# Weights of three projections shifted by 32 bytes in longer buffers, in a decoder layer on one core

## The chip, the cores and the metric

The kernel runs on one core of a Trainium2 chip. The metric is the device time of one execution in microseconds (us); lower is better. A profiled execution gives a trace of every instruction beside that time.

## The reference, cut to what matters

A decoder layer on x of 256 tokens by 1024 features, all in float32:

```
h = rmsnorm(x) ; proj = h @ w_in                       # 1024 -> 3*512 + 512 + 2*1024
q, k, v, u_pool, gate_logits = split(proj)
attn   = causal attention of 8 heads of 64 (one block of 256 tokens), q and k normed and rotated
pooled = causal trailing means of u_pool over 2, 4, 8, 16 tokens, minus the token, a linear map per group
x  = x + (sigmoid(gate_0) * (attn @ w_branch_attn) + sigmoid(gate_1) * (pooled @ w_branch_pool)) @ w_out
up = conv3(rmsnorm(x) @ w_up)                           # 1024 -> 2 * 2816, depthwise, causal
out = x + (silu(gate half of up) * value half of up) @ w_down
```

## The kernel before

Each float32 operand of a large matmul is split in two tiles of type float32r: `hi`, the value rounded (ScalarE, `high`, L80), and `lo`, the rest (VectorE, `low`, L84). A product is then three matmuls: hi by hi, hi by lo, lo by hi. That goes for the weights as well as for the activations.

Weights come in chunks of 128 partitions by 2048 columns (8 KB on each partition), in the order of the list `order` (L97 to L107): q, k, v, p, g, pool, bp, ba, o, up, dn. q's weights come together with x in the tile `xq`; the other chunks are loaded into `raw` buffers by SyncE's queue (`load`). `next_high` and `next_low` split a chunk by pieces, some pieces ahead of TensorE; `next_high` also takes the two tiles for a new chunk, `his[c]` and `los[c]`, from two pools of four buffers each, `whi` and `wlo` (L147 and L148). The sequence of instructions on every engine is the order in which the Python code issues them, and it is kept as written.

Two ways of multiplying matter here:

- `project` (L278) makes q, k and v, token by token: the activation tiles `xhi` and `xlo` are the stationary operand (128x128) and the weights are the moving operand, 512 columns at a time. For each of q, k and v there are 8 steps of k, 3 products and 2 halves of the tokens: 48 matmuls, 144 in all. They come first in the program.
- All other large matmuls (`mm3`, L92 to L94, and `down`, L635 to L637) have the weights as the stationary operand (128x128) and the activations as the moving operand, 256 columns at a time. They are 2460.

Where the tiles lie: each partition holds, one behind the other, the small constants, four `raw` buffers, four `whi`, four `wlo`, and then the activations, of which `xq` is the first. Constants, `raw`, `whi` and `wlo` buffers that matter here begin on a multiple of 64 bytes: `whi` at byte 56768, and each next buffer 8192 further. `xq` has eight columns of `norm_mix_g` (32 bytes) ahead of x and is 24608 bytes long, which is 32 bytes more than a multiple of 64; so x and every activation tile behind it (`xhi` at byte 146912, `xlo`, `qkT`, `vn`, the pooled and attention tiles, those of the FFN) begin 32 bytes behind a multiple of 64. In every float32r matmul of this kernel the two operands so have starts that differ by 32 bytes within 64: the weights at 0, the activations at 32.

Of the kernel before, what the change touches and what calls it, by code (L numbers as in the profile page):

```python
# [9 lines left out]
F32R = mybir.dt.float32r  # L10
# [4 lines left out]
P = 128  # L15
# [17 lines left out]
CH = 2048  # L33
# [19 lines left out]
FFN_AHEAD = 6  # L53
KREADY = 1
FIRST = 2
XCUTS = (1, 2, 4, 6, 8)


@with_exitstack
def hybrid_layer_kernel(ctx: ExitStack, tc: tile.TileContext, xq_d, par_d, wkv_d, wpg_d,  # L60
# [5 lines left out]
    whi_p = ctx.enter_context(tc.tile_pool(name="whi", bufs=WBUFS))  # L66
    wlo_p = ctx.enter_context(tc.tile_pool(name="wlo", bufs=WBUFS))
# [11 lines left out]
    def high(hi, src, scale=1.0):  # L79
        nc.scalar.activation(hi, src, AF.Copy, scale=scale)  # L80
# [16 lines left out]
    order = [("q", None)] * 2 + [("k", wkv_d[c]) for c in range(2)]  # L97
# [10 lines left out]
    raws, his, los = {}, {}, {}  # L108
# [14 lines left out]
    def raw(c, sl):  # L123

        return xq[:, 4 * c + sl.start // 512, S:] if order[c][0] == "q" else raws[c][:, sl]
# [10 lines left out]
    def oldest():  # L136

        return next((c for c in range(len(order)) if c not in spent), len(order))

    def next_high():  # L140
        if at[0] < len(pieces):
            c, sl, first, _ = pieces[at[0]]
            if c - oldest() >= WBUFS:
                return
            at[0] += 1
            if first:
                his[c] = whi_p.tile([P, CH], F32R, tag="whi", name=f"hi_{order[c][0]}{c}")  # L147
                los[c] = wlo_p.tile([P, CH], F32R, tag="wlo", name=f"lo_{order[c][0]}{c}")  # L148
            high(his[c][:, sl], raw(c, sl))

    def next_low(eager=False):
# [9 lines left out]
    def ahead(upto=0):  # L161

        next_high()
        next_low()
        if at[1] - sum(p[0] < used[0] for p in pieces) < upto:
            next_high()
            next_low()
# [23 lines left out]
    cut = 0  # L191
    for k in XCUTS:
        end = KD + k * (S + AW)
# [25 lines left out]
    for k in range(KD):  # L219
        if k == 0:  # L220
            nc.vector.tensor_scalar(xhi[:, k, :], xT[:, k, :], gmix[:, k:k + 1], None, op0=ALU.mult)
        else:
            high(xhi[:, k, :], xT[:, k, :], gmix[:, k:k + 1])
        low(xlo[:, k, :], xhi[:, k, :], xT[:, k, :], gmix[:, k:k + 1])
        next_high()
        next_low(eager=True)
# [83 lines left out]
    def to_heads(qg, t, dst, name):  # L310
        pq = bank(f"ps_t{name}{t}")
        flat = qg.rearrange("p h d -> p (h d)")
        for j in range(KA):
            nc.tensor.transpose(pq[:, j * P:(j + 1) * P], flat[:, j * P:(j + 1) * P], ident)
        nc.scalar.activation(dst[:, :, t * P:(t + 1) * P], pq.rearrange("p (j c) -> p j c", c=P), AF.Copy)
# [110 lines left out]
    def scores(hp):  # L426
        ps = ps2.tile([P, 2, 512], F32, tag="ps2", name=f"ps_s{hp}")
        for j in range(2):
            rows = slice(j * DH, (j + 1) * DH)
            nc.tensor.matmul(ps[:, j, P:3 * P], qT[rows, hp, P:S], kT[rows, hp, :], start=True, stop=True)  # L430
            nc.tensor.matmul(ps[:, j, 0:P], qT[rows, hp, 0:P], kT[rows, hp, 0:P], start=True, stop=True)
        sm = tmp.tile([P, 2, 3 * P], F32, tag="big", bufs=4, name=f"sm{hp}")
        nc.vector.tensor_tensor(sm, ps[:, :, 0:3 * P],
                                mask.rearrange("p a b -> p (a b)")[:, None, :].to_broadcast([P, 2, 3 * P]), ALU.add)
        mx = tmp.tile([P, 2, 2], F32, tag="mx", name=f"mx{hp}")
        for t in (1, 0):
            nc.vector.tensor_reduce(mx[:, t, :], sm[:, :, TOK[t]], axis=AX.X, op=ALU.max)
        nc.vector.tensor_scalar(mx, mx, -(DH ** -0.5), None, op0=ALU.mult)
        sums = tmp.tile([P, 2, 2], F32, tag="sums", name=f"sums{hp}")
        for j in range(2):  # L440
            for t in (1, 0):
                nc.scalar.activation(sm[:, j, TOK[t]], sm[:, j, TOK[t]], AF.Exp, bias=mx[:, t, j:j + 1],
                                     scale=DH ** -0.5, accum_out=sums[:, t, j:j + 1])
        rs = tmp.tile([P, 2, 2], F32, tag="rs", name=f"rs{hp}")
        nc.vector.reciprocal(rs, sums)
        for t in (1, 0):
            n = TOK[t].stop - TOK[t].start
            nc.gpsimd.tensor_tensor(sm[:, :, TOK[t]], sm[:, :, TOK[t]],
                                    rs[:, t, :, None].to_broadcast([P, 2, n]), ALU.mult)
        later(4, weigh, hp, sm)  # L450
# [46 lines left out]
    for n in range(2 * KD):  # L497
        if n == KREADY:
            for t in range(NT):
                to_heads(kg[t], t, kT, "k")  # L500
        if n >= FIRST and (n - FIRST) % 4 == 0:
            scores((n - FIRST) // 4)
        if n == 10:
            pool_maps()
            ahead()
        b, c = n // 2, n % 2
# [267 lines left out]
```

## Time and profile before

| | |
|---|---|
| median of 3 runs | 350.35 us (348.51 to 350.55) |
| profiled execution, its own time | 348.69 us |
| its span, first to last instruction | 346.9 us |
| outside the span | 1.8 us |
| mean granted TensorE clock | 1.000 |

The profile gives for each engine the time it was busy in the span (PE is TensorE's matmuls, PEld its weight loads, DVE VectorE, ACT ScalarE, POOL GpSimd), a strip of 40 slices, the chain of work that ended last, and groups of equal instructions. A matmul's own duration includes a latency that the next matmul overlaps: how fast TensorE gets on is read from the distance between the starts of two matmuls, not from the duration of one.

### The profile page before, as it was taken

To read this page: it belongs to the slowest core of one execution; us is meant where nothing else is said; L and a number is where in the kernel's file an instruction comes from. 1 tells how busy PE (TensorE), PEld (TensorE's weight loads), DVE (VectorE), ACT (ScalarE), POOL (GpSimd) and SP (SyncE) were. 2 spreads that over 40 slices of the span, in tenths; PEclk is the share of its full clock that TensorE was granted. 3 is DMA by queue.
4 is the path that set the end of the run, shared out by engine and by line. 5 is a ranking of instruction groups with operands and counts; after the bars stand their busy time and mean duration, and the time that the engine had idled before them with its cause. 6 is when DMAs were issued, how large, how long until landed. Compare 5 with 4: busy or idle time off the path is not lost.

```text
span 346.9 us, 6715 instructions
## 1 busy us (share of the span) xinstructions
PE 340.7 (98%) x2736; PEld 329.2 (95%) x2736; DVE 261.0 (75%) x411; ACT 195.7 (56%) x311; POOL 101.5 (29%) x111
## 2 busy tenths in 40 slices
PE   8999999999999999999999999999999999999996
PEld 6887899999899999999999999999999999999995
DVE  4969889787587585899699877776777777777643
ACT  4956534634748945665367655555555555646420
POOL 1007991112202034586232212121212121212230
PEclk9999999999999999999999999999999999999999
DMA  7985642465272651566257555464636363652003
GB/s 275 419 327 213 222 159 110 150 220 213 69 259 92 242 201 45 175 237 211 109 168 271 188 224 201 164 222 145 242 123 243 131 235 132 232 162 83 0 2 121
DMA packets 10254, 62.76 MB, mean 181 GB/s; under 512 B 1136, under 2 KB 2288, under 8 KB 3312
## 3 DMA queue, kind: packets, MB, share of 16 engines
q1 hardware_dynamic: 10224, 62.34, 49.5%
q8 instruction: 21, 0.34, 0.4%
q14 instruction: 9, 0.07, 0.1%
HBM read 61.29 MB, written 1.05 MB: 180 GB/s over the span
## 4 chain that ended last, share of the span: by engine, by line
PE 80%; DVE 10%; DMA 4%; ACT 2%; issue 2%; SPq 1%; POOL 0%; ACTq 0%
PE ps_up L93 11%; PE ps_up L94 11%; PE ps_up L92 11%; PE ps_d L636 6%; PE ps_d L637 6%; PE ps_d L635 6%; PE ps_g L92 4%; PE ps_g L94 4%; PE ps_g L93 4%; DMA raw_k<-in_wkv 4%; PE ps_v L278 3%; DVE lo_up L84 2%; DVE hlo L86 2%; PE ps_bp L92 1%; PE ps_ba L94 1%
## 5 line engine op out<-in xcount | busy, mean ns | idle before, releaser
L92 PE MATMUL ps_up<-hhi,hi_up 128*128 128x256 f32 x352 | 98.5, 280 | 0.0
L93 PE MATMUL ps_up<-hlo,hi_up 128*128 128x256 f32 x352 | 98.4, 279 | 0.1
L94 PE MATMUL ps_up<-hhi,lo_up 128*128 128x256 f32 x352 | 98.3, 279 | 0.0
L93 PEld LDWEIGHTS ps_up<-hlo,hi_up 128*128 128x128 f32 x352 | 66.2, 188 | 0.4 <-DVE hlo L86 0.4
L92 PEld LDWEIGHTS ps_up<-hhi,hi_up 128*128 128x128 f32 x352 | 66.2, 188 | 0.0
L94 PEld LDWEIGHTS ps_up<-hhi,lo_up 128*128 128x128 f32 x352 | 66.2, 188 | 0.0
L84 DVE TENSOR_TENSOR lo_up<-raw_up,hi_up 128x1024 fp32r<-128x1024 f32 x44 | 55.9, 1273 | 6.1 <-ACT hi_up L80 6.1
L618 POOL TENSOR_TENSOR c_v<-c_g,c_v 128x256 f32<-128x256 f32 x22 | 16.2, 738 | 120.8 <-DVE c_v L601 120.8
L636 PE MATMUL ps_d<-al,hi_dn 128*128 128x256 f32 x176 | 49.1, 279 | 0.0
L635 PE MATMUL ps_d<-ah,hi_dn 128*128 128x256 f32 x176 | 49.1, 279 | 0.0
L637 PE MATMUL ps_d<-ah,lo_dn 128*128 128x256 f32 x176 | 49.1, 279 | 0.0
L80 ACT ACTIVATE hi_up<-raw_up 128x1024 fp32r<-128x1024 f32 x44 | 44.9, 1045 | 0.0
L92 PE MATMUL ps_g<-xhi,hi_g 128*128 128x256 f32 x128 | 36.5, 285 | 0.0
L93 PE MATMUL ps_g<-xlo,hi_g 128*128 128x256 f32 x128 | 35.7, 279 | 0.0
L94 PE MATMUL ps_g<-xhi,lo_g 128*128 128x256 f32 x128 | 35.7, 279 | 0.0
L80 ACT ACTIVATE ah<-c_v 128x256 fp32r<-128x256 f32 x22 | 9.2, 418 | 45.8 <-POOL c_v L618 45.8
L637 PEld LDWEIGHTS ps_d<-ah,lo_dn 128*128 128x128 f32 x176 | 33.1, 188 | 0.0
L635 PEld LDWEIGHTS ps_d<-ah,hi_dn 128*128 128x128 f32 x176 | 33.1, 188 | 0.0
L636 PEld LDWEIGHTS ps_d<-al,hi_dn 128*128 128x128 f32 x176 | 33.1, 188 | 0.0
L606 DVE TENSOR_TENSOR u_v<-ps_up,R 128x256 f32<-128x256 f32 x22 | 9.3, 421 | 26.1 <-PE ps_up L94 26.1
L84 DVE TENSOR_TENSOR lo_dn<-raw_dn,hi_dn 128x1024 fp32r<-128x1024 f32 x22 | 27.8, 1264 | 0.4 <-ACT hi_dn L80 0.4
L642 POOL TENSOR_TENSOR al<-c_v,ah 128x256 fp32r<-128x256 f32 x22 | 23.0, 1045 | 11.6 <-ACT ah L80 11.6
(182 smaller groups left out, 815.8 us busy)
## 6 DMA issues: line engine op xcount, KB each, us to landing
raw_up<-in_wup SPq DMA_DIRECT2D x22, 1024.0 KB, 4.8
raw_dn<-in_wdn SPq DMA_DIRECT2D x11, 1024.0 KB, 4.8
raw_g<-in_wpg SPq DMA_DIRECT2D x8, 1024.0 KB, 4.8
raw_o<-in_wout SPq DMA_DIRECT2D x4, 1024.0 KB, 4.8
xq<-in_xq SPq DMA_DIRECT2D x3, 768.0 KB, 7.4
raw_v<-in_wkv SPq DMA_DIRECT2D x2, 1024.0 KB, 14.1
raw_p<-in_wpg SPq DMA_DIRECT2D x2, 1024.0 KB, 6.3
raw_bp<-in_wbp SPq DMA_DIRECT2D x2, 1024.0 KB, 4.8
```

Source lines behind the costliest of these rows:

```text
L80: nc.scalar.activation(hi, src, AF.Copy, scale=scale)
L84: nc.vector.tensor_tensor(lo, src, hi.bitcast(F32), ALU.subtract)
L92: nc.tensor.matmul(out, sh, mh, start=start, stop=False, **kw)
L93: nc.tensor.matmul(out, sh, ml, start=False, stop=False, **kw)
L94: nc.tensor.matmul(out, sl, mh, start=False, stop=stop, **kw)
L278: nc.tensor.matmul(pt[t], sx[:, k, t * P:(t + 1) * P], wx[:, sl], start=k == 0 and sx is xhi and wx is hi, stop=k == KD - 1 and wx is lo)
L606: nc.vector.tensor_tensor(u, ps[:, 0:S], R2, ALU.mult)
L618: nc.gpsimd.tensor_tensor(uc[1], g[1], uc[1], ALU.mult)
L635: nc.tensor.matmul(o, hi[:, sl], acch[i], start=first, stop=False, skip_group_check=True)
L636: nc.tensor.matmul(o, hi[:, sl], accl[i], start=False, stop=False, skip_group_check=True)
L637: nc.tensor.matmul(o, lo[:, sl], acch[i], start=False, stop=i == KF - 1, skip_group_check=True)
L642: nc.gpsimd.tensor_tensor(accl[i], act_i, acch[i].bitcast(F32), ALU.subtract)
```

## The change

`BEHIND` is a number of float32 columns. The tiles of all weights are made 16 columns (64 bytes) longer, and for chunks of q, k and v the part that is used begins 8 columns (32 bytes) behind the tile's start; all others use the tile from its start.

```
+BEHIND = 8
...
             if first:
-                his[c] = whi_p.tile([P, CH], F32R, tag="whi", name=f"hi_{order[c][0]}{c}")
-                los[c] = wlo_p.tile([P, CH], F32R, tag="wlo", name=f"lo_{order[c][0]}{c}")
+                name = order[c][0]
+                off = BEHIND if name in ("q", "k", "v") else 0
+                his[c] = whi_p.tile([P, CH + 2 * BEHIND], F32R, tag="whi", name=f"hi_{name}{c}")[:, off:off + CH]
+                los[c] = wlo_p.tile([P, CH + 2 * BEHIND], F32R, tag="wlo", name=f"lo_{name}{c}")[:, off:off + CH]
             high(his[c][:, sl], raw(c, sl))
```

No instruction is added, removed or moved on any engine, and no wait: row for row the two programs differ in nothing but their source lines, which are 1 higher after L56 and 3 more after L148 (L80 becomes L81, L278 becomes L282). Nor does a tile change its buffer. What changes is where they lie. The eight weight buffers follow each other by 8256 bytes in place of 8192, so that all still begin on a multiple of 64; `xq` and all tiles behind it move up by 512 bytes (`xhi` from 146912 to 147424) and still begin 32 bytes behind a multiple of 64. q's, k's and v's weights now begin at 32 too, as the stationary tiles `xhi` and `xlo` do that they are multiplied with. For the other 2460 matmuls the operands stay 32 bytes apart within 64, but their distance in whole steps of 64 bytes changes, by between 1 and 8 steps, by the buffer.

## Rows read from the trace of the kernel before

**Rows 1.** The page: busy time of each engine, and the granted clock by slices.
```profile
PE 340.7 (98%) x2736; PEld 329.2 (95%) x2736; DVE 261.0 (75%) x411; ACT 195.7 (56%) x311; POOL 101.5 (29%) x111
...
PEclk9999999999999999999999999999999999999999
```
**Rows 2.** The page: the chain that ended last, by engine.
```profile
PE 80%; DVE 10%; DMA 4%; ACT 2%; issue 2%; SPq 1%; POOL 0%; ACTq 0%
```
**Rows 3.** Waits of TensorE's matmuls: total us, times, longest.
```profile
PE ps_warm L204 <- DVE ones L178: 1.0, 1, 1.0
PE ps_s L430 <- ACT qkT L315: 0.5, 1, 0.5
PE ps_q L278 <- ACT hi_q L80: 0.4, 2, 0.3
PE ps_n L249 <- DVE diag L245: 0.4, 1, 0.4
PE ps_v L278 <- DVE qg_q L291: 0.3, 1, 0.3
```
**Rows 4.** Timeline of TensorE, q to p: start us, us, instruction, count.
```profile
9.77 0.63 PE L278 MATMUL ps_q<-lo_q,xhi 128*128 128x512 f32 x2
...
17.24 0.63 PE L278 MATMUL ps_k<-hi_k,xhi 128*128 128x512 f32 x2
...
28.84 0.63 PE L278 MATMUL ps_k<-lo_k,xhi 128*128 128x512 f32 x2
29.31 0.40 PE L278 MATMUL ps_v<-hi_v,xhi 128*128 128x512 f32 x1
30.02 0.47 PE L278 MATMUL ps_v<-hi_v,xhi 128*128 128x512 f32 x1 [0.31 <-DVE qg_q L291]
30.33 0.63 PE L278 MATMUL ps_v<-hi_v,xlo 128*128 128x512 f32 x2
...
40.59 0.63 PE L278 MATMUL ps_v<-lo_v,xhi 128*128 128x512 f32 x2
41.06 0.28 PE L92 MATMUL ps_u<-xhi,hi_p 128*128 128x256 f32 x1
```
**Rows 5.** Timeline of TensorE in the FFN's up projection, 15 steps of three.
```profile
200.66 0.28 PE L92 MATMUL ps_up<-hhi,hi_up 128*128 128x256 f32 x1
...
205.92 0.28 PE L92 MATMUL ps_up<-hhi,hi_up 128*128 128x256 f32 x1
```
**Rows 6.** Groups: matmuls and weight loads; the first number behind the bar is busy us, then mean ns.
```profile
L93 PE MATMUL ps_up<-hlo,hi_up 128*128 128x256 f32 x352 | 98.4, 279 | 0.1
...
L93 PEld LDWEIGHTS ps_up<-hlo,hi_up 128*128 128x128 f32 x352 | 66.2, 188 | 0.4 <-DVE hlo L86 0.4
...
L635 PE MATMUL ps_d<-ah,hi_dn 128*128 128x256 f32 x176 | 49.1, 279 | 0.0
...
L278 PE MATMUL ps_v<-lo_v,xhi 128*128 128x512 f32 x16 | 5.0, 396 | 0.0
...
L278 PEld LDWEIGHTS ps_v<-lo_v,xhi 128*128 128x128 f32 x16 | 3.0, 188 | 0.7
```
**Rows 7.** Writers of four weight tiles and two activation tiles: ns min/median/max, first and last start.
```profile
L84 DVE TENSOR_TENSOR lo_q<-xq,hi_q x8: 684/685/693, 5.2 to 13.7; 128x512 fp32r<-128x512 f32 x8
L84 DVE TENSOR_TENSOR lo_k<-raw_k,hi_k x4: 1216/1218/1225, 14.4 to 22.6; 128x1024 fp32r<-128x1024 f32 x4
L84 DVE TENSOR_TENSOR pooll<-pl,poolh x4: 393/418/421, 53.5 to 67.5; 128x256 fp32r<-128x256 f32 x4
L80 ACT ACTIVATE hi_q<-xq x8: 615/616/629, 4.4 to 12.8; 128x512 fp32r<-128x512 f32 x8
L80 ACT ACTIVATE hi_k<-raw_k x4: 1042/1044/1061, 13.3 to 19.0; 128x1024 fp32r<-128x1024 f32 x4
L80 ACT ACTIVATE ah<-c_v x22: 417/418/419, 170.9 to 335.6; 128x256 fp32r<-128x256 f32 x22
```

## The prediction

> **What bounds the kernel now.** I read the busy times first, then the chain that ended last, then TensorE's waits, and last the starts of single matmuls. TensorE's matmuls cover 340.7 of 346.9 us, at a granted clock that the strip shows as 9 tenths or more in every slice [rows 1], which is the level of 2.4 GHz; 80% of the chain is TensorE's [rows 2]. Its waits are few: five rows of 0.3 to 1.0 us, and only two of them, 0.4 us for q's first weights and 0.3 us at v's start, lie in the part where q, k and v are made [rows 3]. So the time is the number of matmuls times the distance between their starts, and a change of that distance is what could move it.
>
> That distance is read from starts. In q's last 32 matmuls it is (17.24 - 9.77) / 32 = 233.4 ns; in v's last 46 it is (41.06 - 30.33) / 46 = 233.3 ns [rows 4]. In the up projection it is (205.92 - 200.66) / 45 = 116.9 ns [rows 5]. The first kind moves 512 columns, the second 256, so both take 0.456 ns for a column. At the granted 2.4 GHz a column of one cycle would take 0.417 ns (512 of them 213.3 ns): each matmul carries 9% above that, 20 ns in 512 columns and 10 ns in 256.
>
> **The change, part by part.**
>
> *The start of the moving operand.* This is the part that could work on TensorE directly: 144 matmuls read their moving operand, the weights, from 32 bytes behind a multiple of 64 in place of 0. The kernel before has both cases side by side: weights that move in q, k and v start at 0 [rows 4], activations that move in the up projection start at 32 [rows 5], and a column takes the same 0.456 ns. The mean durations say the same by another way: 396 ns for 512 columns less 279 ns for 256 is 117 ns for 256 columns [rows 6]. The 9% grows with the columns and not with the matmuls, so it is not an extra line at the start that another offset would save or add. Term: 144 x 0 ns = 0.
>
> *The pair of starts.* What no row of before shows is a float32r matmul whose two operands start alike within 64 bytes; after the change q, k and v are such. Bounds from both sides: at best the 9% goes from all 144, 144 x 20 = 2.9 us; at worst each load of a stationary tile, now hidden under the matmul ahead of it, has to be waited for, 144 x 188 ns = 27 us [rows 6]. I take 0, the value nearest to the rows: a load takes 188 ns whether its tile starts at 0 (ps_up) or at 32 (ps_v), and if loads and moving reads disturbed each other, the excess would come once for each load; but a matmul of 512 columns has one load just as one of 256 has, and twice the excess.
>
> *The writers.* ScalarE and VectorE now write 16 pieces each of q, k and v at offset 32. VectorE takes 684 ns for 512 columns with a source at 32 and the rest at 0, and 1218 ns for 1024 with everything at 0: the difference, 534 ns, is that of 512 columns, so what is left for the start is 151 ns in both. With all three tiles at 32 the fastest of 256 columns is 393 ns and the median 418, again some 151 ns above half of 534 [rows 7]. ScalarE: 1044 less 616 ns is 428 ns for 512 columns and leaves 188 ns for the start; 256 columns from 32 to 32 took 418 ns, which leaves 204 [rows 7]. So at most 16 ns on 16 pieces, 0.26 us, on an engine that is busy 56% of the span [rows 1] and that delayed q's matmuls twice by 0.4 us together [rows 3]. Only the first pieces of q, with x just arriving, are uncovered. Term: 0 to 0.05 us.
>
> *The longer buffers.* The 2460 other matmuls keep their operands 32 bytes apart within 64, and only whole steps of 64 bytes between them change. They are most of the time, so a nanosecond on each would be 2.5 us. Bounds: the whole excess gone or doubled, 2460 x 10 = 24.6 us either way. I take 0: ps_up and ps_d read different activation tiles against all the weight buffers, and both have 279 ns [rows 6]. That is weak, since by the addresses all these distances are whole kilobytes and 32 bytes; what speaks more for 0 is again that the excess follows the columns and not the loads.
>
> No instruction, queue or wait moves, so nothing is late in another place. Sum against the profiled execution: 348.69 + 0 (0 to 0.05). That execution lies 1.7 us under the median of the runs, inside their spread of 348.51 to 350.55; I forecast the median, unchanged: **350.3 us**, its own range 348.4 to 351.0.
>
> **The rivals.**
>
> *A: operands that start alike lose the excess.* The 144 matmuls then come every 213 ns. For it: 20 ns on each are unexplained by the columns at the granted clock, and every pair that shows them starts 32 bytes apart. Against it: two opposite arrangements, 0 against 32 and 32 against 0, give one and the same 0.456 ns. The gain would mostly be lost again: in q and k together it is at most 96 x 20 = 1.9 us, but v's second matmul starts at 30.02 when VectorE has cleared the bank of q's second half [rows 4, 3], and VectorE's sequence does not get earlier. What is sure is v's part, 46 x 20 = 0.9 us: 350.35 - 0.9 = 349.4, and 347.4 if the wait fell too.
>
> The Trainium skill states for it, in "TensorE: Matmul & The Clock Gate", section "Wait — 56ns, not 53.3ns?", that warm matmuls start N / 2.4 + 2.5 ns apart, 215.8 ns at 512 columns, which the page measured with another type. The trace disagrees, with 233.3 ns. If the page's distance came back with the new start, the gain would be 17.5 ns on each, 0.8 us for v's 46.
>
> *B: operands that start alike get into each other's way.* The load for the next matmul runs while this one moves its columns; with the same phase both could ask for the same part of the memory in the same cycle. Place: the 144 matmuls of q, k and v. Price: if the load's 128 columns each cost the moving side one column's time, 128 x 0.417 = 53 ns, 144 x 53 = 7.7 us, so 358.0. It decides from 24 ns a matmul (3.5 us). For it: the pair is new in this kernel. Against it: the excess does not come once per load, as told.
>
> The Trainium skill speaks against it too: "SBUF — State Buffer", section "Who interferes with whom", gives TensorE two read ports, one for the moving operand and one for weight loads, independent of each other. By that the price is 0. That loads of 188 ns at 116.9 ns between matmuls cost no more per column than at 233.3 agrees; a pair in phase is shown by no run here.
>
> *C: whole steps of 64 bytes count.* Then the longer buffers change the 2460 others, and the sign is open: 1 ns on each is 2.5 us, 352.8 or 347.9; it decides from 1.4 ns. For it: their number. Against it: the equal rows of ps_up and ps_d, as far as they go, and that the excess does not follow the loads.
>
> **How the numbers follow.** No change 0.74; A 0.10; B 0.07; C 0.09. One per cent, about what a measurement of this kernel can tell from no change, is 3.5 us. A stays below it by its own arithmetic, but for 0.02 together with a low draw of the runs; C gives 0.04 to each side; of B 0.06 is above the bound. Faster by over 1%: 0.02 + 0.04 = 0.06. Slower: 0.06 + 0.04 = 0.10. Within 1%: 0.84. The range reaches down to A's better end and, for a weak B or C, up to 353: 347.5 to 353.0. It leaves out most of B and of C, some 0.14.
>
> **What would show it.** Right: matmuls of q, k and v still 233 ns apart, those of the up projection 117, loads at 188, and v's start at about 30 us with its wait on VectorE. A would show as 213 to 216 ns in q, k and v, with a longer wait at v's start; B as 250 ns or more there, with p starting later than 41 us; C as a distance other than 117 ns in the FFN, perhaps in one buffer of four. The forecast is wrong if any of these distances moved by more than 2%.

## The result, and the profile after

| | before | after |
|---|---|---|
| median | 350.19 us (348.44 to 350.59, 8 runs) | 351.88 us (351.77 to 352.11, 8 runs) |
| ratio, 95% interval | | 1.0062 (1.0043 to 1.0081) |
| span of the profiled execution | 346.9 us | 350.2 us |

The change is slower by some 0.6%. That is less than the 1% that the prediction took for what a measurement can tell from no change, and yet it is clear of noise, since the interval does not hold 1. One thing is needed to read the sizes: the kernel before has two times, one near 348.7 and one near 350.3 us, and its median falls on one or the other by the set of runs; the changed kernel has one time. The profiled execution of before was one of the shorter (348.69 us), so that the two profiles differ by 3.3 us where these medians differ by 1.7. The ratios, here and below, weigh the runs of both times and so are not the quotients of the medians beside them. Where the two times come from is shown by the ninth experiment.

The page of the changed kernel, busy times and granted clock:

```profile
PE 344.0 (98%) x2736; PEld 332.6 (95%) x2736; DVE 261.1 (75%) x411; ACT 195.7 (56%) x311; POOL 102.1 (29%) x111
...
PEclk9999999999999999999999999999999999999999
```

Against [rows 1], TensorE is busy 3.3 us longer, which is the whole difference of the spans, and VectorE, ScalarE and GpSimd are busy as long as before, within 0.6 us. The clock is the same. So TensorE's own work became longer. Its waits in the changed kernel (us in total, times, longest) add up to 2.9 us where those of [rows 3] add up to 2.6. The difference lies at q's first weights, and it is made up again before p starts, as the timeline below shows:

```profile
PE ps_warm L207 <- DVE ones L181: 1.1, 1, 1.1
PE ps_q L281 <- ACT hi_q L81: 0.7, 2, 0.4
PE ps_s L433 <- ACT qkT L318: 0.4, 1, 0.4
PE ps_v L281 <- DVE qg_q L294: 0.4, 1, 0.4
PE ps_n L252 <- DVE diag L248: 0.3, 1, 0.3
```

The timeline of TensorE from q to p (start us, us, instruction, count), the part whose tiles were shifted. L281 is L278 of the kernel before: the lines behind L148 are 2 higher, not 3, than those ahead of it, and the section on the change is wrong there.

```profile
9.82 0.62 PE L281 MATMUL ps_q<-lo_q,xhi 128*128 128x512 f32 x2
...
17.26 0.62 PE L281 MATMUL ps_k<-hi_k,xhi 128*128 128x512 f32 x2
...
29.23 0.40 PE L281 MATMUL ps_v<-hi_v,xhi 128*128 128x512 f32 x1
30.01 0.47 PE L281 MATMUL ps_v<-hi_v,xhi 128*128 128x512 f32 x1 [0.39 <-DVE qg_q L294]
...
30.78 0.62 PE L281 MATMUL ps_v<-lo_v,xhi 128*128 128x512 f32 x2
...
34.86 0.62 PE L281 MATMUL ps_v<-lo_v,xhi 128*128 128x512 f32 x2
...
35.78 0.63 PE L281 MATMUL ps_v<-hi_v,xlo 128*128 128x512 f32 x2
...
40.91 0.28 PE L93 MATMUL ps_u<-xhi,hi_p 128*128 128x256 f32 x1
```

The reader sees no loss here but a small gain: p starts at 40.91 us, 0.15 earlier than in [rows 4]. In v's first chunk matmuls start (34.86 - 30.78) / 18 = 226.7 ns apart, in its second (40.91 - 35.78) / 22 = 233.2; before it was 233.3 in both. One and the same kind of matmul, with the same shift, has two speeds, and what differs between the two chunks is the buffer, and with it the distance from the start of the moving tile to that of the stationary tile: modulo 256 bytes it is 0 in the first chunk and 64 in the second. Within 64 bytes the operands begin alike in both, so that alone does not make them faster.

The timeline of the FFN, for chunks 31, 33, 34, 36 and 37 of the list `order` (all of the up projection): the first matmul of a chunk and the one 48 further, in pairs:

```profile
193.43 0.28 PE L93 MATMUL ps_up<-hhi,hi_up 128*128 128x256 f32 x1
199.11 0.28 PE L638 MATMUL ps_d<-ah,hi_dn 128*128 128x256 f32 x1
...
201.91 0.28 PE L93 MATMUL ps_up<-hhi,hi_up 128*128 128x256 f32 x1
207.54 0.28 PE L638 MATMUL ps_d<-ah,hi_dn 128*128 128x256 f32 x1
...
210.35 0.28 PE L93 MATMUL ps_up<-hhi,hi_up 128*128 128x256 f32 x1
216.10 0.28 PE L638 MATMUL ps_d<-ah,hi_dn 128*128 128x256 f32 x1
...
218.94 0.28 PE L93 MATMUL ps_up<-hhi,hi_up 128*128 128x256 f32 x1
224.70 0.29 PE L638 MATMUL ps_d<-ah,hi_dn 128*128 128x256 f32 x1
...
227.55 0.28 PE L93 MATMUL ps_up<-hhi,hi_up 128*128 128x256 f32 x1
233.15 0.28 PE L638 MATMUL ps_d<-ah,hi_dn 128*128 128x256 f32 x1
```

By the 48 steps of each pair that is 118.3, 117.3, 119.8, 120.0 and 116.7 ns (starts are shown to 10 ns, so such a mean is good to 0.2 ns). In the kernel before all five have 116.7; here chunk 34 of that kernel:

```profile
209.06 0.28 PE L92 MATMUL ps_up<-hhi,hi_up 128*128 128x256 f32 x1
214.66 0.28 PE L635 MATMUL ps_d<-ah,hi_dn 128*128 128x256 f32 x1
```

Put beside the addresses of the built program the five values are a table by buffer. The distance below is the start of the stationary weight tile minus that of the moving activation tile, modulo 256 bytes; before it is 224 for all.

| hi buffer | distance, after | chunk | ns from start to start |
|---|---|---|---|
| first (56768, as before) | 224 | 37 | 116.7 |
| second (65024) | 32 | 31 | 118.3 |
| third (73280) | 96 | 33 and 36 | 117.3 and 120.0 |
| fourth (81536) | 160 | 34 | 119.8 |

The third buffer's two values are not scatter. From chunk 30 to chunk 54 each of its chunks runs between the two halves of a down chunk: where that one lies in the second buffer (chunks 36, 45 and 54) the third has 120.0 ns, and where it lies in the first or the fourth (30, 33, 39, 42, 48 and 51) it has 117.3 or 117.4.

So the time did not come from q, k and v. It came from the matmuls that the shift leaves alone, by the 64 bytes that the buffers grew. The groups answer to [rows 6]: the mean of the up projection's matmuls went from 279 to 281 ns, that of v's third product from 396 to 391, and a weight load takes 189 ns where it took 188:

```profile
L94 PE MATMUL ps_up<-hlo,hi_up 128*128 128x256 f32 x352 | 98.9, 281 | 0.0
...
L94 PEld LDWEIGHTS ps_up<-hlo,hi_up 128*128 128x128 f32 x352 | 66.5, 189 | 0.2 <-DVE hlo L87 0.2
...
L281 PE MATMUL ps_v<-lo_v,xhi 128*128 128x512 f32 x16 | 5.0, 391 | 0.0
```

### The profile page after: what moved, and what is told of

It is laid out like the page before. It is cut to its first block, busy times and chain, and to the rows that moved or that the text cites. A ratio compares the mean times of both kernels' runs of the same rounds, so it can differ in the third digit from the quotient of the medians.

```text
span 350.2 us, 6715 instructions
## 1 busy us (share of the span) xinstructions
PE 344.0 (98%) x2736; PEld 332.6 (95%) x2736; DVE 261.1 (75%) x411; ACT 195.7 (56%) x311; POOL 102.1 (29%) x111
## 4 chain that ended last, share of the span: by engine, by line
PE 80%; DVE 10%; DMA 3%; ACT 2%; issue 2%; SPq 1%; POOL 0%; ACTq 0%
PE ps_up L95 11%; PE ps_up L94 11%; PE ps_up L93 11%; PE ps_d L640 6%; PE ps_d L639 6%; PE ps_d L638 6%; PE ps_g L93 4%; PE ps_g L95 4%; PE ps_g L94 4%; DMA raw_k<-in_wkv 3%; PE ps_v L281 3%; DVE lo_up L85 2%; DVE hlo L87 2%; PE ps_bp L93 1%; PE ps_bp L95 1%
## 5 line engine op out<-in xcount | busy, mean ns | idle before, releaser
L81 ACT ACTIVATE hi_up<-raw_up 128x1024 fp32r<-128x1024 f32 x44 | 44.9, 1045 | 0.0
L81 ACT ACTIVATE ah<-c_v 128x256 fp32r<-128x256 f32 x22 | 9.2, 418 | 45.7 <-POOL c_v L621 45.7
```

## The experiments

The theory (T): for a given moving tile, the time from one float32r matmul to the next depends on the distance, modulo 256 bytes, between the moving tile and the stationary tile that is loaded while it moves. The rivals: the shifted start of q, k and v costs (S); longer or unevenly spaced buffers cost by themselves (L). Every kernel below computes the whole reference. All are edits of the kernel before.

**e1_growth_alone.**

```
-...whi_p.tile([P, CH], F32R, ...)
+...whi_p.tile([P, CH + 16], F32R, ...)[:, 0:CH]
 (the same for wlo)
```

> The tiles of all weights are 64 bytes longer as in the changed kernel, and nothing begins 32 bytes behind. Theory T (what counts is the distance, modulo 256 bytes, between the moving tile and the stationary tile that is loaded meanwhile; in the changed kernel's trace matmuls of 256 columns start 116.7 ns apart at a distance of 224, 118.4 at 32, 118.2 at 96 and 119.9 at 160): the FFN keeps the four distances of the changed kernel, 576 x 1.7 + 767 x 1.5 + 540 x 3.2 ns = 3.9 us over the profiled execution of before, so 352.5, and buffers of the FFN with means of 116.7, 118.3, 117.4 to 120.0 and 119.9 ns. Rival S (the shifted start of q, k and v is what costs): 350.2 and 116.7 ns in every buffer.

Measured: 351.98 us (351.92 to 352.05), against 348.72 for the kernel before in the same set; ratio 1.0074 (1.0051 to 1.0098). That is the time of the changed kernel, 351.88, without any shift. Its FFN is the changed kernel's, here chunks 31 and 34 (timeline of TensorE, first matmul and 48 further): 118.1 and 120.0 ns.

```profile
193.48 0.28 PE L92 MATMUL ps_up<-hhi,hi_up 128*128 128x256 f32 x1
199.15 0.28 PE L635 MATMUL ps_d<-ah,hi_dn 128*128 128x256 f32 x1
...
210.39 0.28 PE L92 MATMUL ps_up<-hhi,hi_up 128*128 128x256 f32 x1
216.15 0.28 PE L635 MATMUL ps_d<-ah,hi_dn 128*128 128x256 f32 x1
```

The growth is the cause, and S falls. It says nothing yet on T against L.

**e2_shift_alone.**

```
+off = 8 if order[c][0] in ("q", "k", "v") else 0
-...whi_p.tile([P, CH], F32R, ...)
+...whi_p.tile([P, CH + 64], F32R, ...)[:, off:off + CH]
 (the same for wlo)
```

> q, k and v begin 32 bytes behind as in the changed kernel, but the tiles grow by 256 bytes, so that for all other matmuls the distance modulo 256 is that of before. Theory T: 116.7 ns in every buffer of the FFN, q, k and v at 229 ns in place of 233 (the changed kernel's matmuls of 512 columns at distance 0), 144 x 4 = 0.6 us at most, part of it lost at v's wait: 349.6 to 350.2. Rival S: 351.9. If the distance counts beyond 256 bytes, the FFN's buffers differ from each other.

Measured: 348.82 us (348.69 to 350.65), ratio 0.9997 (0.9978 to 1.0015): no change. The buffers are longer by 256 bytes and nothing is lost, so length by itself is not it. The timeline of TensorE: q to p, then chunk 34 of the FFN.

```profile
9.77 0.62 PE L279 MATMUL ps_q<-lo_q,xhi 128*128 128x512 f32 x2
...
17.03 0.61 PE L279 MATMUL ps_k<-hi_k,xhi 128*128 128x512 f32 x2
...
28.88 0.40 PE L279 MATMUL ps_v<-hi_v,xhi 128*128 128x512 f32 x1
29.95 0.47 PE L279 MATMUL ps_v<-hi_v,xhi 128*128 128x512 f32 x1 [0.68 <-DVE qg_q L292]
...
40.73 0.28 PE L92 MATMUL ps_u<-xhi,hi_p 128*128 128x256 f32 x1
...
209.17 0.28 PE L92 MATMUL ps_up<-hhi,hi_up 128*128 128x256 f32 x1
214.77 0.28 PE L636 MATMUL ps_d<-ah,hi_dn 128*128 128x256 f32 x1
```

In the FFN it is 116.7 ns again, with buffers 8448 bytes apart: a growth by 256 bytes leaves the distance modulo 256, and the speed, as they were. In q the last 32 matmuls start (17.03 - 9.77) / 32 = 226.9 ns apart in place of 233.4, so operands that begin alike (distance 0) are faster here. Where that gain goes can be read in two waits: v begins 0.43 us earlier than in [rows 4] but its second matmul only 0.07, since it waits for VectorE to clear a bank (0.68 us in place of 0.31); p begins 0.33 earlier, and then the first scores wait longer for ScalarE (us in total, times, longest):

```profile
PE ps_s L431 <- ACT qkT L316: 0.9, 1, 0.9
PE ps_v L279 <- DVE qg_q L292: 0.7, 1, 0.7
```

In [rows 3] these were 0.5 and 0.3.

**e3_gap64 and e4_gap32.** Buffers as in the kernel before; between the pools of weights and activations lies an unused tile of 64 (e3) or 32 (e4) bytes:

```
+gap = ctx.enter_context(tc.tile_pool(name="gap", bufs=1)).tile([P, 16], F32, name="gap")   # e4: [P, 8]
 act = ctx.enter_context(tc.tile_pool(name="act", bufs=1))
```

> All buffers as before; an unused tile of 64 bytes lies between the weights and the activations, so that the distance is 160 in all 2460 matmuls with stationary weights. Theory T: 119.9 ns everywhere, 2460 x 3.2 = 7.9 us, so 356.6 over the profiled execution, 358 over the median. Rival L (longer or unevenly spaced buffers cost, by themselves): 350.2.

> An unused tile of 32 bytes in the same place: both operands of all float32r matmuls begin alike within 64 bytes, at distance 192. No row shows 256 columns at such a distance. If the gain of the changed kernel's 512 columns (233 to 230 at 192, 2 ns for 256 columns) holds: 2460 x 1.5 = 3.7 us less, 346. If only whole steps of 64 count: 350. If operands that start alike disturb each other (the prediction's rival B) by more: above 352.

Measured: e3 355.69 us (355.62 to 355.79), ratio 1.0175 (1.0145 to 1.0205); e4 350.76 us (350.39 to 350.94), ratio 1.0046 (1.0031 to 1.0062). In e3 no buffer is longer and every address of a weight is that of before; 64 unused bytes cost 7 us. Chunk 34 in e3:

```profile
212.17 0.28 PE L93 MATMUL ps_up<-hhi,hi_up 128*128 128x256 f32 x1
217.93 0.28 PE L636 MATMUL ps_d<-ah,hi_dn 128*128 128x256 f32 x1
```

That is 120.0 ns, as in the changed kernel's buffer at the same distance of 160 (119.8). There the weights had moved and here the activations did, so it is the distance that counts and not the place of either. L falls, T stands. In e4 the hope for 346 was wrong: the gain of 512 columns at distance 192 does not carry over to 256 columns, which have 117.7 ns there (chunk 34, from 209.99 to 215.64 us).

**e5_gap224, e6_gap96, e7_gap160 and e8_all16.** The other distances in steps of 32 with both operands beginning alike, by gaps of 224, 96 and 160 bytes in the same place, and one of 16 bytes by the edit of e2 with `off = 4` for all chunks.

> All buffers as before, an unused tile of 224 bytes between the weights and the activations: distance 0 modulo 256 in all 2604 float32r matmuls. Theory T with the value that 512 columns had at distance 0 in the kernel with the shift alone (227.5 ns, so 113.8 for 256): 2460 x 2.9 = 7.2 us less than before, 341.5, if VectorE keeps up. If the distance acts on 256 columns otherwise (one load for each 256, two for the time of 512): anything from 115 to 120 ns, 344.6 to 356.8.

> The same with 96 bytes: distance 128 in the 2460. The changed kernel's 512 columns had 232.2 ns there, 116.1 for 256: about 1.5 us less than before, 347. If 256 columns behave as at 192 (117.7 ns): 351.

> The same with 160 bytes: distance 64 in the 2460, 192 in q, k and v. The changed kernel's 512 columns had 233.3 ns at 64, as before: 348.7. If 256 columns behave as at 192 (117.7 ns): 351.

> All weights begin 16 bytes behind their buffers, which grow by 256 bytes: distance 240 in the 2460 and 16 in q, k and v. If the distance acts in steps of 32 or 64 bytes alone, 116.7 or the value at 0; if it acts smoothly, a value between those of 224 and 0 (between 116.7 ns and that of the run with 224 bytes in between).

Measured, with chunk 34 from each timeline (its first matmul, and 48 further):

| run | distance | chunk 34, us | ns | time, us | ratio to before |
|---|---|---|---|---|---|
| e5 | 0 | 211.98 to 217.74 | 120.0 | 355.41 | 1.0184 (1.0163 to 1.0205) |
| e6 | 128 | 211.07 to 216.77 | 118.8 | 352.98 | 1.0130 (1.0095 to 1.0164) |
| e7 | 64 | 208.52 to 214.17 | 117.7 | 349.03 (342.85 to 349.61) | see below |
| e8 | 240 | 209.94 to 215.57 | 117.3 | 354.27 (350.30 to 354.93) | 1.0107 (1.0064 to 1.0149) |

e5 is the clearest miss: distance 0 is the best found for 512 moving columns and level with the worst for 256, in one and the same execution (q's second chunk, 24 matmuls from 11.69 to 17.13 us, has 226.7 ns), so no value can be carried from one of the two kinds of matmul to the other. One run of e6 took 355.07 us, the others 353.0. e8 shows that 16 bytes count (117.3 ns at 240, between 116.7 at 224 and 120.0 at 0), but its times fall in two groups, four at 350.3 to 350.5 and six at 354.2 to 354.9: the 117.3 ns are of the shorter group, from which the profile is, and its median is of the longer, of which there is no profile. e7 has two as well: eight runs at 348.8 to 349.6 and three at 342.85 to 343.25; its ratio, 0.9823 (0.9787 to 0.9858), is that of the three alone. Its profile, one of the longer runs, holds both speeds in one execution: chunks 27 and 31 of the up projection, each by its first matmul and the one 48 further. Both lie in the second buffer and are multiplied with the same activations.

```profile
169.40 0.28 PE L93 MATMUL ps_up<-hhi,hi_up 128*128 128x256 f32 x1
174.84 0.28 PE L93 MATMUL ps_up<-hhi,hi_up 128*128 128x256 f32 x1
...
191.56 0.28 PE L93 MATMUL ps_up<-hhi,hi_up 128*128 128x256 f32 x1
197.21 0.28 PE L636 MATMUL ps_d<-ah,hi_dn 128*128 128x256 f32 x1
```

That is 113.3 and 117.7 ns at one and the same distance. So a distance does not set one value: it allows one or two patterns, and a stream of matmuls can stay in the one that it fell into. T had to be widened by that. Here the stream goes over in chunk 30, at a start that comes 0.23 us behind the one ahead of it (184.62 and 184.85 us); what held it up there the profile does not show.

**e9_before_again.** The kernel before without an edit, to see its longer time.

> The kernel before, unchanged. Its runs have two times, some 348.7 and some 350.3. If the two are two patterns into which the starts of the matmuls fall at one and the same distance (as the run with 160 bytes in between shows with 113.3 and 117.8 ns in one execution), a profile at 350.3 shows 117 ns or more in a long stretch, with nothing else later; if something else makes the second time, all matmuls are 116.7 ns apart and the 1.6 us lie in waits.

Measured: 350.35 us. The profile fell on the longer time, and chunk 34 shows it:

```profile
209.41 0.28 PE L92 MATMUL ps_up<-hhi,hi_up 128*128 128x256 f32 x1
215.06 0.28 PE L635 MATMUL ps_d<-ah,hi_dn 128*128 128x256 f32 x1
```

117.7 ns, where the profile of before has 116.7. From chunk 27 on all have 117.7 or 117.8 by their starts, which over the 175 us left is 1.6 us. By these two profiles the two times of the kernel before are two patterns at one distance; they part in chunk 26, where small matmuls of the norm (ps_n) interrupt the stream in both.

**e10_lo_sweep and e11_hi_sweep.** The gap of 160 bytes, and 64 bytes more for the lo tiles alone (e10) or the hi tiles alone (e11), so that each buffer is another pair of distances.

```
+...wlo_p.tile([P, CH + 16], F32R, ...)[:, 0:CH]     # e10; e11: whi_p
+gap = ...tile([P, 40], F32, name="gap")
```

> 160 bytes in between, and the lo tiles alone are 64 bytes longer: hi tiles at distance 64, lo tiles at 64, 128, 192 or 0 by the buffer. If each load counts by its own distance, a third of the matmuls (those beside the load of a lo tile) go from the value at 64 (113.3 or 117.8 ns) to those found at 128, 192 and 0 (118.8, 117.7, 120.0): buffers with means of (2 x 113.3 + 118.8) / 3 = 115.1, 114.8 and 115.5, or 118.1, 117.8 and 118.5 where the slow pattern holds. Total between 344 and 350.

> 160 bytes in between, and the hi tiles alone are 64 bytes longer: lo tiles at distance 64, hi tiles at 64, 128, 192 or 0 by the buffer. By the same rule two thirds change: (113.3 + 2 x 118.8) / 3 = 117.0 at 128, 116.2 at 192, 117.8 at 0. Total between 346 and 351; if buffers at one distance hold the fast pattern throughout, that distance is the one to take.

Measured: e10 347.33 us (347.27 to 347.44), ratio 0.9932 (0.9906 to 0.9958); e11 350.35 us (350.20 to 350.72), ratio 1.0026 (1.0008 to 1.0045), with the kernel before at 350.25, its longer time, in this set. The totals lie in the expected ranges, but the rule that each load counts by itself does not hold. In e10, chunks 31 and 33, lo tiles at 128 and at 192:

```profile
191.48 0.28 PE L93 MATMUL ps_up<-hhi,hi_up 128*128 128x256 f32 x1
197.15 0.28 PE L636 MATMUL ps_d<-ah,hi_dn 128*128 128x256 f32 x1
...
199.98 0.28 PE L93 MATMUL ps_up<-hhi,hi_up 128*128 128x256 f32 x1
205.45 0.28 PE L636 MATMUL ps_d<-ah,hi_dn 128*128 128x256 f32 x1
```

118.1 and 114.0 ns, where the rule gave 115.1 and 114.8 in the fast pattern or 118.1 and 117.8 in the slow. Chunk 31 could be the rule's slow pattern; what the rule can't give is the mirror of chunk 33 in e11, hi tiles at 192 and lo tiles at 64: there chunk 33 (200.86 to 206.56 us) has 118.8 ns, where the rule gave 116.2. The pair of hi at 64 and lo at 192 is fast in every chunk of e10 that has it; the other three pairs are slow there or change between both.

**e12_hi64_lo192.** That pair in every buffer, by 128 unused bytes between the hi and the lo pool and 32 between the lo pool and the activations; no buffer is longer.

```
 whi_p = ...
+gap0 = ctx.enter_context(tc.tile_pool(name="gap0", bufs=1)).tile([P, 32], F32, name="gap0")
 wlo_p = ...
+gap = ctx.enter_context(tc.tile_pool(name="gap", bufs=1)).tile([P, 8], F32, name="gap")
 act = ...
```

> All buffers of the length of before; 128 unused bytes between the hi and the lo tiles and 32 between the lo tiles and the activations: for the 2460 matmuls hi tiles at distance 64, lo tiles at 192, in every buffer. In the run with lo tiles at four distances this pair had means of 113.4 to 114.6 ns in all its 16 chunks, without a slow pattern. Theory T: some 113.9 ns everywhere, 2460 x 2.8 = 6.9 us less than 348.7 where VectorE keeps up: 342 to 343, with little spread. If the pair held only because of what its neighbours left behind: 346 or more, or two times as in the run with 160 bytes.

Measured: 342.53 us (342.40 to 342.80), against 348.64; ratio 0.9819 (0.9800 to 0.9838). Faster than both kernels, by 160 bytes that nobody reads, and with no second time in its five runs. Chunk 34, 113.3 ns:

```profile
206.99 0.28 PE L94 MATMUL ps_up<-hhi,hi_up 128*128 128x256 f32 x1
212.43 0.28 PE L637 MATMUL ps_d<-ah,hi_dn 128*128 128x256 f32 x1
```

Of the 2460 x (116.7 - 113.3) = 8.4 us that this speed is worth, 6.1 arrive. Part of the rest is in TensorE's waits, which grew: the first scores and the up projection's first tiles now wait for other engines.

```profile
PE ps_s L432 <- ACT qkT L317: 1.0, 1, 1.0
PE ps_up L95 <- DVE hlo L88: 0.7, 1, 0.7
```

## Why the prediction was wrong, point by point

- *What bounds the kernel.* Right: the time is the number of matmuls times the distance between their starts, and all of the change lies there. The forecast of 350.3 came within 1% of 351.88, and its range held it, but that was luck in part: it was put on the longer of the two times of the kernel before, while its working rested on a profile of the shorter. Against that profile's time the change costs 3.2 us (351.88 - 348.69).
- *The longer buffers.* This is the step that failed: "I take 0", on the ground that ps_up and ps_d have one duration and that the excess follows the columns and not the loads. Measured alone (e1) it is 3.3 us. The text had seen why its rows could not decide: all distances in the kernel before are alike in their low bits (whole kilobytes and 32 bytes). The rows then show one point of a curve, and 279 ns twice is one value measured twice. Rival C had the mechanism and the place, buffers of four that differ, and put its deciding point at 1.4 ns a matmul; the FFN's 26 chunks from 31 to 56 lost 1.7 ns a matmul, and over all 2460 the 3.3 us are 1.3 ns each, just under that point.
- *The excess does not come once per load, so loads and moving reads do not disturb each other.* Wrong as an argument. The excess over 0.417 ns a column was taken as a fixed property of the stream. It depends on where the stationary tile lies from the moving one: 113.3 to 120.0 ns for 256 columns over the runs above. That the same share stood at 256 and at 512 columns in the kernel before was a coincidence of its distances: at distance 0 a column takes 0.469 ns in the one (e5) and 0.443 in the other (e2).
- *The start of the moving operand, the pair of starts.* The total of q, k and v was taken as 0 and is nearly that in time (e2: ratio 0.9997), for two reasons that the prediction gave to rival A: beginning alike does make these matmuls faster, 226.9 ns in q of e2 at distance 0, but 233.2 in v's second chunk of the changed kernel at 64, and nowhere the 213 that A named; and the gain of q and k is lost at v's second matmul, which waits for VectorE until 29.95 us. The part of v, which A held to be sure, is lost as well, at the first scores. In the changed kernel only v's first chunk reached 226.7 ns. Rival B is refuted for these 512-column matmuls, which were at 233.4 ns or less at each of the changed kernel's distances 0, 64, 128 and 192; for 256 columns, which the change does not bring to distance 0, e5 shows a loss of 3.3 ns a matmul.
- *The pages that were cited.* "SBUF — State Buffer", section "Who interferes with whom", of the Trainium skill calls TensorE's two reads independent; with every instruction, tile size and weight address unchanged, e3 loses 7 us by a move of the activations by 64 bytes alone. For float32r the time so depends on how the two tiles lie to each other, and the measurement decides; whether the two reads are what meets there is not shown. The distance of 215.8 ns for 512 columns in "TensorE: Matmul & The Clock Gate", section "Wait — 56ns, not 53.3ns?", of the Trainium skill was reached by no run here; the nearest was 226.7.
- *The writers.* Right in its bound: VectorE's and ScalarE's busy times are those of before, their shifted pieces of q and k take 682 and 1220 ns (VectorE) and 617 and 1044 ns (ScalarE), and p starts earlier, not later. (The 151 ns for the start are 150 by the figures beside them, which changes nothing.)
- *What would show it.* The prediction called itself wrong if a distance moved by more than 2%, and some did: 120.0 and 119.8 ns in place of 116.7 in the third and fourth buffers, and 226.7 in place of 233.3 in v's first chunk. The loads (187 to 189 ns) and v's start (30.01 us, with its wait for VectorE) came as forecast.

What is left open is what in the memory makes the distances differ, and what decides which of two patterns a stream falls into, beyond what was seen: the chunk around it in the third buffer, an interruption in e7 and e9. The profiles show the starts alone; a clash of the two reads is the nearest reading, but it was not measured by itself.

## What to carry to other kernels

Where TensorE is the bound and the start-to-start time of float32r matmuls, the only type tried here, lies above one column a cycle, treat the distance between stationary and moving tiles as a parameter: put a few unused bytes between the pools, try steps of 32 or 64 up to 256, and read the starts by buffer. A buffer that grows by a few bytes moves everything behind it; grow it by 256, or compensate. And a row that repeats in every group is evidence only for the conditions that differ between the groups: look first whether the quantity in question differs at all.

## What the runs showed that was not expected

- Unused bytes between pools changed this kernel between 342.53 (e12) and 355.69 us (e3), 3.8%, with the same instructions in the same order.
- One kernel at one distance runs in two stable patterns: 116.7 and 117.7 ns in the kernel before, 113.3 and 117.7 at distance 64, 117.3 and 120.0 in the third buffer of the changed kernel. What looked like a spread of the measurement, 348.44 to 350.59 us, is these two, as far as one profile of each shows.
- The best distance is not the same for the two kinds of matmul: distance 0 gave 226.9 ns for 512 moving columns and 120.0 for 256. They differ in more than their columns, since the weights move in the one and are stationary in the other.
